# Second attention of a two-block model: seven of eighteen key tiles as float32 products, the other eleven split from PSUM

## Chip, cores and metric

The kernel runs on one NeuronCore of a Trainium2 chip. The metric is the time of one execution on the device, in microseconds (us); for the kernel before it is the median of three runs.

## What is computed

The model has two blocks over 2048 tokens of width 1024, all in float32. Block 1 joins a latent attention and a state space part. Block 2 joins a grouped-query attention with a retention and ends in a mixture of 32 experts. Only the attention of block 2 matters here: 8 query heads of width 64 share 2 key heads, and each query looks at 256 context keys and 2048 token keys, which is 2304 keys or 18 tiles of 128.

```python
def _attend(q, k, v):
    qb = jnp.moveaxis(q.reshape(B, nb, Q_BLOCK, ATTN_KV_HEADS, GQA_GROUP, HEAD_DIM), 1, 0)
    scale = HEAD_DIM ** -0.5
    def one_block(q_blk):
        s = jnp.einsum('bqhgd,bkhd->bhgqk', q_blk, k).astype(jnp.float32) * scale
        p = jax.nn.softmax(s, axis=-1)
        return jnp.einsum('bhgqk,bkhd->bqhgd', p.astype(v.dtype), v)
```

## The kernel before

Stages run one after another: `phase_a`, `phase_qkv`, `phase_attn1` (613 to 1262 us), the state space part's output and `Mix`, `phase_b` (projections of block 2), `phase_attn2` (about 2108 to 3190 us), `phase_out2`, `phase_moe`, `phase_end`.

Most products run in a format called float32r, which keeps the upper bits of a float32 and takes one pass over TensorE. A float32 operand is therefore split in a high part (a cast) and a low part (the operand less its high part, by a subtraction), and a product is put together from the passes that matter. A product of two plain float32 operands is also possible; the profile records it as two MATMUL instructions, each with a weight load of its own.

`Attention2` works through 32 units. A unit is 128 queries of the four heads that share keys, so its moving operands have 512 columns. For each unit:

- `top` finds the maxima of the next unit's scores: 20 products `pa` (16 of 512 columns, 4 of 256, L1161), each reduced by VectorE out of PSUM into `nm` (L1162, two buffers of `pa`). Then a small reduction `mx`, four transposes into a bank of the pool `a2t` and a ScalarE copy make a row of `qm`, which the scores of the next unit need.
- For each of the 18 key tiles, `scores` makes two products into a PSUM tile `ps` (L1182, L1183; two buffers). `exps` takes the exponential on ScalarE from PSUM into an SBUF tile `p` (L1187) and casts it to the high part `ph`, also on ScalarE (L1191). `rest` subtracts to get the low part `pl` (L1199): nine tiles on VectorE, nine on GpSimd. All three operands lie in SBUF.
- The sums over the keys are the softmax's denominators. The string `ACC` says how the high parts enter them. For ten tiles TensorE multiplies `ph` by a column of ones (L1236). For the other eight VectorE adds `ph` to `accD`, seven additions per unit (L1209); `fold` splits the result in `sumh` (ScalarE) and `suml` (VectorE, L319), and two more products with ones bring it in.
- `values` comes five tiles later (`LAG`): `o` += (high and low parts of the values) times `ph` (L1232), and `o1` += (ones, high parts of the values) times `pl` (L1238). Row 0 of `o1` gathers the sum.
- `finish` takes `o` and `o1` out of PSUM (one buffer each, L1247 to L1250), sends the sum through memory to get its reciprocal onto all rows, and multiplies on GpSimd (L1254, L1265).

In the gaps, `Retention.steps` takes one step at the tiles named in `SIDE`, four in a unit. Each step uses a bank of the pool `a2t`, which has two. A chunk's steps include four small VectorE operations with SBUF operands in a row, twice: `rst` at L1049 and `on` at L1076. There are 16 chunks.

PSUM has eight banks, and the stage uses all: `pa` 2, `ps` 2, `o` and `o1`, `a2t` 2. The order of instructions on each engine is made by a planner that follows the order of the code but fills in what it holds to be ready; each engine then works its own queue strictly in order.

Of the kernel before, what the change touches and what calls it, by code (L numbers as in the profile page):

```python
# [10 lines left out]
F = mybir.dt.float32  # L11
R = mybir.dt.float32r
# [3 lines left out]
OP = mybir.AluOpType  # L16
# [17 lines left out]
class K:  # L34
    """What every part of the kernel shares: the core, the arguments, constants, small helpers."""
# [27 lines left out]
    def tr(self, out, x):  # L63
        """out = x transposed, bit for bit."""
        self.nc.tensor.transpose(out, x, self.ident)  # L65

    def rsqrt(self, out, src, n):
        """out = (src / n + eps) ** -0.5 on small tiles."""
        nc = self.nc
        nc.vector.tensor_scalar(out, src, 1.0 / n, EPS, op0=OP.mult, op1=OP.add)  # L70
        w = out.free_size()
        nc.gpsimd.tensor_tensor(out, out, self.mhalf[: out.partition_size(), :w], op=OP.pow)  # L72

    def reduce_angle(self, x, k):
        """x -> x - 2 pi round(x / 2 pi), within [-pi, pi]; k: room of x's shape."""
# [8 lines left out]
    def sin_cos(self, pool, s, c, x, shape):  # L84
        """s, c = sin(x), cos(x); x is spent."""
# [8 lines left out]
    def cmul(self, pool, ore, oim, are, aim, bre, bim, shape, neg_im=False, second=None):  # L94
        """(ore + i oim) = a b, elementwise; with neg_im, oim = -Im(a b)."""
# [16 lines left out]
# Chunks of 16 tokens. Lanes of the tables: (direction, state). A table of powers has 17 entries e:  # L112
# lambda^e forward, lambda^(16 - e) backward.
# [3 lines left out]
def early(k):  # L117
    """What rests on the parameters alone, in small parts."""
# [56 lines left out]
        # Powers 0..16, ascending for both directions: [lanes, e, g].  # L175
# [16 lines left out]
        # Bbar = (lambda_bar - 1) / lambda B  # L192
# [18 lines left out]
        # Tables with e in the direction's order; pw: lambda^s' forward, lambda^(15 - s') backward.  # L211
# [10 lines left out]
        # Bbar with columns (direction, h), zero off its direction.  # L222
# [10 lines left out]
        # The skip weights, on the diagonal of lag 0: rows 32 j + h of a batch of two groups.  # L233
# [72 lines left out]
def mm3(nc, out, lh, ll, rh, rl, start, stop):  # L306
    """out (+)= (lh + ll)^T (rh + rl) in three passes; the product of the low parts is below float32."""
# [5 lines left out]
def split(nc, hi, lo, src, eng=None):  # L313
    """src = hi + lo exactly, each of 12 bits."""
# [13 lines left out]
class Proj:  # L328
    """Rows of a normalized matrix, transposed and split, against weights that stream through."""
# [18 lines left out]
    def half_block(self):  # L348
        """Room of up to two tiles, in that of the last block's low parts."""
# [4 lines left out]
    def add_rows(self, blk, i, x):  # L354
        """Tile i of four of a block: x [128 rows, 1024]."""
# [8 lines left out]
    def weights(self, c0, n, w=None, upto=8):  # L364
        """Columns of the weights, split; w: the rows that are there already."""
# [12 lines left out]
    def rows(self, blk, i, w, n):  # L378
        """PSUM [128 rows of tile i, n]."""
# [6 lines left out]
    def cols(self, blk, w, m):  # L386
        """PSUM [128 columns of weight tile m, 512 rows]."""
# [7 lines left out]
def norm_rows(k, pool, out, x, g, n, b=None):  # L395
    """out = x / rms(x) * g (+ b) over n columns."""
# [73 lines left out]
def rope_tables_1(k):  # L470
    """[c, s, (cos, cos)] and [c, s, (-sin, sin)] of 32 frequencies, to memory. Yields after each small part."""
# [140 lines left out]
class Attention:  # L612
    """For each head and 128 queries: scores with the queries on partitions, their maximum, the
    exponentials, their transposes split in two; for 256 queries the products with the values
    (stationary). The parts of neighbouring tiles of queries alternate as `order` says."""
# [25 lines left out]
    def start(self, n):  # L641
        """The tile n of queries and what it holds."""
# [20 lines left out]
    def M(self, t, j):  # L663
        """The scores times -scale, in place, and the running minimum."""
# [43 lines left out]
    def D(self, t, g, copy=None):  # L708
        """A group that stays whole, for products in float32."""
# [6 lines left out]
    def Y(self, t, g):  # L716
        """Split from the copy: the high part here, the low part on the engine that has time."""
# [6 lines left out]
    def P(self, b):  # L724
        """A share of a block's products with the values."""
# [22 lines left out]
    def X(self, b):  # L748
        """One over the sums, on all partitions."""
# [39 lines left out]
class Attention1(Attention):  # L789
# [4 lines left out]
    def setup(self, ctx):  # L794
        k, nc = self.k, self.nc
        k.at = k.scratch("at", [4, 128, S])            # normalized outputs, features on partitions
# [4 lines left out]
        # The next phase's loads go to the room of the even heads, which is free first.  # L801
# [9 lines left out]
    def load_part(self, h, c):  # L811
        """One of eight parts of a head's keys and values, if it isn't there yet."""
# [78 lines left out]
def decay_tables(k):  # L891
    """Tables of the decays, to memory: the retention's fac, gc, dm and gn. Yields after each small part."""
    nc, a = k.nc, k.a
    k.dec = k.scratch("dec", [128, 9 * HR + 2 * HR + HR * 128])
    with ExitStack() as ctx:
# [4 lines left out]
        # log of the decays: -log(1 + exp(-x)), as min(x, 0) - log(1 + exp(-|x|)).  # L900
# [12 lines left out]
        # Distances on partitions: p + 1, 128 - p, 127 - p, p; and 255 - p, 127 - p, p, 128 + p.  # L913
# [5 lines left out]
        # Factors [128, head, direction]: of the queries; of the keys, with 1/8; of the context's keys.  # L919
# [7 lines left out]
        # Over a chunk, on the state's partitions (direction, dk).  # L927
# [4 lines left out]
        # Decays of the scores [key j, head, query i], with 1/8.  # L932
# [20 lines left out]
class Retention:  # L953
    def constants(self, k, cp):
        """Tables of the decays."""
        self.k = k
        k.rsb = k.scratch("rsb", [NT, 64, 512])        # states of the backward direction before each chunk
        k.ruf = k.scratch("ruf", [NT, 64, 512])        # what each chunk adds to the forward state
# [3 lines left out]
    def spread(self, wk, x, j, name):  # L962
        """[row, head, direction, 64]: x [row, (head, 64)] times factor j."""
# [128 lines left out]
class Attention2:  # L1092
# [92 lines left out]
    def exps(self, u, t):  # L1185
# [4 lines left out]
        if self.HI[t] == "A":  # L1190
            self.nc.scalar.copy(hi, p)  # L1191
# [1287 lines left out]
```

## Time and profile before

| | us |
|---|---|
| median of three runs | 4474.56 |
| lowest and highest of them | 4474.19, 4477.1 |
| span of the profiled execution | 4460.7 |
| median less span | 13.9 |
| TensorE busy over the span | 4063.1 |
| VectorE busy | 3244.0 |
| ScalarE busy | 2301.0 |
| GpSimd busy | 1988.3 |

The page gives busy times of the whole span. The stage of the second attention is about a quarter of it, so the views that count are those of this stretch alone: from the first handing over of a unit's sum (2168.9 us) to the last (3190.6 us) there are 31 units. The profile records the matmuls' ends by a model, so that durations of matmuls that follow each other overlap; the distance between their starts says what one costs.

### The profile page before, as it was taken

To read this page: it belongs to the slowest core of one execution; us is meant where nothing else is said; L and a number is where in the kernel's file an instruction comes from. 1 tells how busy PE (TensorE), PEld (TensorE's weight loads), DVE (VectorE), ACT (ScalarE), POOL (GpSimd) and SP (SyncE) were. 2 spreads that over 40 slices of the span, in tenths; PEclk is the share of its full clock that TensorE was granted. 3 is DMA by queue.
4 is the path that set the end of the run, shared out by engine and by line. 5 is a ranking of instruction groups with operands and counts; after the bars stand their busy time and mean duration, and the time that the engine had idled before them with its cause. 6 is when DMAs were issued, how large, how long until landed. Compare 5 with 4: busy or idle time off the path is not lost. (4 is left out here: it accounts for less than half of the span.)

```text
span 4460.7 us, 60030 instructions
## 1 busy us (share of the span) xinstructions
PE 4063.1 (91%) x19842; PEld 3214.7 (72%) x19842; DVE 3244.0 (73%) x5326; ACT 2301.0 (52%) x4166; POOL 1988.3 (45%) x2239
## 2 busy tenths in 40 slices
PE   7999889999988989999888888989898799999997
PEld 5777768888876878887666666666587677777775
DVE  7563368887625365534999999999765778888886
ACT  3233455555524343322667777777521556666664
POOL 3430078882003422222555555555300566666664
PEclk9999989999998999999999999999999899999998
DMA  5543852331253464334421111110352788888885
GB/s 142 169 146 109 280 192 74 92 112 53 66 160 123 132 206 127 121 103 135 117 71 52 50 45 43 50 41 25 96 172 95 265 279 280 284 280 275 277 282 184
DMA packets 432999, 647.63 MB, mean 145 GB/s; under 512 B 88576, under 2 KB 228096, under 8 KB 432428
## 3 DMA queue, kind: packets, MB, share of 16 engines
q1 hardware_dynamic: 403868, 562.67, 39.9%
q0 software_dynamic: 21840, 66.25, 4.2%
q10 hardware_dynamic: 6976, 14.85, 1.0%
q8 instruction: 157, 2.57, 0.2%
q14 instruction: 158, 1.29, 0.1%
HBM read 496.33 MB, written 156.10 MB: 146 GB/s over the span
## 5 line engine op out<-in xcount | busy, mean ns | idle before, releaser
L1199 POOL TENSOR_TENSOR pl<-p,ph 128x512 fp32r<-128x512 f32 x288 | 416.1, 1450 | 244.8 <-ACT ph L1191 189.4
L2251 DVE TENSOR_TENSOR wlo<-raw,whi 128x1024 fp32r<-128x1024 f32 x256 | 471.6, 1855 | 66.1 <-ACT whi L2248 66.0
L2248 ACT CAST whi<-raw 128x1024 fp32r<-128x1024 f32 x384 | 394.9, 1048 | 130.9 <-DMA raw<-in_moe_w_up 43.9
L1162 DVE TENSOR_REDUCE nm<-pa 128x1 f32<-128x512 f32 (+1 forms) x640 | 390.0, 623 | 19.7 <-PE pa L1161 18.4
L1187 ACT ACTIVATE p<-ps 128x512 f32<-128x512 f32 x576 | 333.2, 599 | 105.6 <-PE ps L1183 87.0
L1161 PE MATMUL pa<-kk,q 128*128 128x512 f32 (+1 forms) x640 | 266.3, 425 | 95.7 <-DVE nm L1162 85.1
L1191 ACT CAST ph<-p 128x512 fp32r<-128x512 f32 x576 | 342.6, 624 | 7.7
L2251 POOL TENSOR_TENSOR wlo<-raw,whi 128x1024 fp32r<-128x1024 f32 x128 | 319.6, 2504 | 53.5 <-ACT whi L2248 47.4
L310 PE MATMUL z<-wh,hlo 128*128 128x512 f32 (+2 forms) x816 | 304.7, 374 | 0.0
L308 PE MATMUL z<-wh,hhi 128*128 128x512 f32 (+2 forms) x768 | 291.4, 381 | 7.5 <-DVE zo L455 2.4
L309 PE MATMUL z<-wl,hhi 128*128 128x512 f32 (+2 forms) x768 | 289.4, 377 | 2.7 <-DVE wl L319 2.7
L72 POOL TENSOR_TENSOR nr<-nr,mhalf 128x1 f32<-128x1 f32 x98 | 61.7, 631 | 499.2 <-DVE nr L70 441.1
L1199 DVE TENSOR_TENSOR pl<-p,ph 128x512 fp32r<-128x512 f32 x288 | 275.4, 956 | 9.8 <-ACT ph L1191 8.3
L1161 PEld LDWEIGHTS pa<-kk,q 128*128 128x128 f32 x640 | 124.0, 195 | 198.4 <-DVE nm L1162 167.0
L1182 PE MATMUL ps<-q,kk 128*128 128x512 f32 x576 | 241.5, 420 | 0.3
L661 PE MATMUL s<-kn,q 128*128 128x512 f32 x768 | 230.0, 407 | 10.0 <-ACT p L674 5.7
L1238 PE MATMUL o<-pl,v 128*128 128x512 f32 x544 | 220.4, 409 | 17.3 <-DVE pl L1199 12.6
L1232 PE MATMUL o<-ph,v 128*128 128x512 f32 x576 | 233.0, 407 | 2.7 <-DVE oc L1249 2.5
L1183 PE MATMUL ps<-qm,kl 65*128 65x512 f32 x576 | 229.0, 407 | 0.2
L1209 DVE TENSOR_TENSOR accD<-accD,ph 128x512 f32<-128x512 f32 x192 | 224.7, 1170 | 0.3
L693 ACT CAST ph<-pt 128x512 fp32r<-128x512 f32 x256 | 142.8, 596 | 151.1 <-PE pt L65 147.8
L697 DVE TENSOR_TENSOR pl<-pt,ph 128x512 fp32r<-128x512 f32 x256 | 167.9, 685 | 67.4 <-ACT ph L693 66.8
(634 smaller groups left out, 11924.5 us busy)
## 6 DMA issues: line engine op xcount, KB each, us to landing
raw<-in_moe_w_gate SPq DMA_DIRECT2D x128, 512.0 KB
raw<-in_moe_w_up SPq DMA_DIRECT2D x128, 512.0 KB
raw<-in_moe_w_down SPq DMA_DIRECT2D x128, 512.0 KB
raw<-in_w_in SPq DMA_DIRECT2D x136, 256.0 KB
w<-in_w_ada SPq DMA_DIRECT2D x96, 256.0 KB
xt<-in_x SPq DMA_DIRECT2D x32, 512.0 KB
xt<-x SPq DMA_DIRECT2D x28, 512.0 KB
rv<-rv SPq DMA_DIRECT2D x34, 256.0 KB
```

The costliest lines, as they stand in the source:

```text
L308: nc.tensor.matmul(out, lh, rh, start=start, stop=False)
L309: nc.tensor.matmul(out, lh, rl, start=False, stop=False)
L310: return nc.tensor.matmul(out, ll, rh, start=False, stop=stop)
L1161: nc.tensor.matmul(pa[:, :c1 - c0], q[:, h], kk[:, c0:c1], start=True, stop=True)
L1162: nc.vector.tensor_reduce(nm[:, h, c:c + 1], pa[:, :c1 - c0], axis=AX.X, op=OP.max)
L1182: nc.tensor.matmul(ps, kk[:, ts], q, start=True, stop=False)
L1187: self.nc.scalar.activation(p, u["s"].pop(t), AF.Exp, scale=self.scale)
L1191: self.nc.scalar.copy(hi, p)
L1199: (nc.vector if self.LO[t] == "D" else nc.gpsimd).tensor_tensor(lo, p, hi.bitcast(F), op=OP.subtract)
L1232: nc.tensor.matmul(u["o"], v[:, t, 64:], hi, start=first, stop=last)
L2248: nc.scalar.copy(hi, raw)
L2251: i = eng.tensor_tensor(lo, raw, hi.bitcast(F), op=OP.subtract)
```

## The change

Seven key tiles, `WHOLE2`, keep their exponentials whole. Their `p` meets the values in one float32 product, with ones and values side by side as the stationary operand (`vw`), so that sum and output come from the same product. There is no cast, no subtraction and no addition for them.

The other eleven, `SPLIT2`, write their exponential back into the PSUM tile it came from. The cast reads PSUM, and the subtraction, now always on VectorE, reads PSUM and the high part. The high parts of these tiles are added up on GpSimd (`acc`, ten additions per unit), and one float32 product with a stationary operand of 128 columns (ones in the first, zeros elsewhere) brings the sum into `o1`. The products with single columns of ones, `accD` and `fold` go.

PSUM is dealt out anew: `ps` has three buffers, `a2t` one. `TOP` moves the three places where two maxima's products fall into one tile. `phase_b` writes the values of the seven tiles whole (64 columns) and those of the others split, into two scratch tensors, which the stage loads with one more transfer per key head.

```diff
+WHOLE2 = (2, 4, 7, 9, 12, 14, 17)
+SPLIT2 = tuple(t for t in range(NT + 2) if t not in WHOLE2)
 class Attention2:
-    TOP = (1, 1, 1, 1, 2, 1, 1, 1, 2, 1, 1, 1, 2, 1, 1, 1, 1, 1)
+    TOP = (1, 1, 1, 2, 1, 1, 2, 1, 2, 1, 1, 1, 1, 1, 1, 1, 1, 1)
-    HI = "AAAAAAAAAAAAAAAAAA"
-    LO = "DPDPDPDPDPDPDPDPDP"
-    ACC = "EDEDEDEDEDEDEDEDEE"      # which one adds up the high parts
-    ROW = "A"
...
-        self.pS = ctx.enter_context(k.pool("a2s", 2, space=PSUM))
+        self.pS = ctx.enter_context(k.pool("a2s", 3, space=PSUM))
-        self.pT = ctx.enter_context(k.pool("a2t", 2, space=PSUM))
+        self.pT = ctx.enter_context(k.pool("a2t", 1, space=PSUM))
-        self.ones = cp.tile([128, 1], R, name="on1")
-        nc.vector.tensor_copy(self.ones, k.ones[:, 0:1])
+        self.one = cp.tile([128, 128], F, name="on1")
+        nc.vector.memset(self.one, 0.0)
+        nc.vector.memset(self.one[:, 0:1], 1.0)
...
-            v = cp.tile([128, self.NK, 192], R, name=f"v{g}")         # ones, high and low parts
+            v = cp.tile([128, len(SPLIT2), 192], R, name=f"v{g}")
+            vw = cp.tile([128, len(WHOLE2), 128], F, name=f"vw{g}")
...
+            nc.sync.dma_start(vw[:, :, 64:], k.v2w[g].rearrange("t p n -> p t n"))
-            nc.gpsimd.tensor_copy(v[:, :, 0:64], k.ones[:, None, 0:64].to_broadcast([128, self.NK, 64]))
+            nc.gpsimd.tensor_copy(v[:, :, 0:64], k.ones[:, None, 0:64].to_broadcast([128, len(SPLIT2), 64]))
+            nc.gpsimd.tensor_copy(vw[:, :, 0:64], k.ones[:, None, 0:64].to_broadcast([128, len(WHOLE2), 64]))
...
     def exps(self, u, t):
-        p = self.wk.tile([128, 512], F, name="p", bufs=5)
-        self.nc.scalar.activation(p, u["s"].pop(t), AF.Exp, scale=self.scale)
+        ps = u["s"].pop(t)
+        if t in WHOLE2:
+            u["p"][t] = p = self.wk.tile([128, 512], F, name="p", bufs=5)
+            self.nc.scalar.activation(p, ps, AF.Exp, scale=self.scale)
+            return
+        self.nc.scalar.activation(ps, ps, AF.Exp, scale=self.scale)
         hi = self.wk.tile([128, 512], R, name="ph", bufs=self.RING)
-        u["p"][t] = [p, hi]
-        if self.HI[t] == "A":
-            self.nc.scalar.copy(hi, p)
+        self.nc.scalar.copy(hi, ps)
+        u["p"][t] = ps, hi
 
     def rest(self, u, t):
...
+        if t in WHOLE2:
+            return
+        ps, hi = u["p"][t]
         lo = self.wk.tile([128, 512], R, name="pl", bufs=self.RING)
-        (nc.vector if self.LO[t] == "D" else nc.gpsimd).tensor_tensor(lo, p, hi.bitcast(F), op=OP.subtract)
+        nc.vector.tensor_tensor(lo, ps, hi.bitcast(F), op=OP.subtract)
         u["p"][t] = hi, lo
...
-                acc = had[0] if had[1] else self.wk.tile([128, 512], F, name="acc" + e, bufs=1)
-                eng.tensor_tensor(acc, had[0], hi.bitcast(F), op=OP.add)
-                u["acc"][e] = acc, True
-            if t == max(self.ACC.rfind(x) for x in "DP"):
-                self.fold(u)
...
+        if t == SPLIT2[0]:
+            u["acc"] = hi.bitcast(F)
+        else:
+            acc = u["acc"] if t > SPLIT2[1] else self.wk.tile([128, 512], F, name="acc")
+            nc.gpsimd.tensor_tensor(acc, u["acc"], hi.bitcast(F), op=OP.add)
+            u["acc"] = acc
 
     def values(self, u, t):
...
-        nc.tensor.matmul(u["o"], v[:, t, 64:], hi, start=first, stop=last)
-        if first:
-            nc.tensor.matmul(u["o1"], v[:, t, 0:128], lo, start=True, stop=False)
-        for x in ([hi] if self.ACC[t] == "E" else []) + (u["sum"] if last and "sum" in u else []):
-            nc.tensor.matmul(u["o1"][0:1], self.ones, x, start=False, stop=False)
-        if not first:
-            nc.tensor.matmul(u["o1"], v[:, t, 0:128], lo, start=False, stop=last)
+        if last:
+            nc.tensor.matmul(u["o1"], self.one, u["acc"], start=False, stop=False)
+        if t in WHOLE2:
+            nc.tensor.matmul(u["o1"], vw[:, WHOLE2.index(t)], p, start=False, stop=last)
+        else:
+            hi, lo = p
+            j = SPLIT2.index(t)
+            nc.tensor.matmul(u["o"], v[:, j, 64:], hi, start=first, stop=t == SPLIT2[-1])
+            nc.tensor.matmul(u["o1"], v[:, j, 0:128], lo, start=first, stop=last)
...
     def do_kv(z, s):
-            vt = wk.tile([128, 2, 2, 64], R, name="vt")
...
+            if kt in WHOLE2:
+                vw = wk.tile([128, 2, 64], F, name="vt")
+                nc.scalar.copy(vw, v)
+                nc.sync.dma_start(k.v2w[:, WHOLE2.index(kt)].rearrange("h p n -> p h n"), vw)
+            else:
+                vt = wk.tile([128, 2, 2, 64], R, name="vt")
+                split(nc, vt[:, :, 0], vt[:, :, 1], v)
```

## Rows read from the trace of the kernel before

**Rows 1.** The page: span, busy time of each engine, VectorE in 40 slices.
```profile
span 4460.7 us, 60030 instructions
...
PE 4063.1 (91%) x19842; PEld 3214.7 (72%) x19842; DVE 3244.0 (73%) x5326; ACT 2301.0 (52%) x4166; POOL 1988.3 (45%) x2239
...
DVE  7563368887625365534999999999765778888886
```
**Rows 2.** One line's instructions: count; ns min/median/max; first and last start.
```profile
L1248 DVE COPY ow<-o x32: 669/672/680, 2168.9 to 3190.6; 1x512 f32<-1x512 f32 x32
```
**Rows 3.** Stretch by engine: us; PE, PEld, DVE, ACT, POOL busy; clock; DMA; GB/s.
```profile
2168.90:3190.60 1021.70, 907.02 (x3985) 631.31 (x3983) 996.08 (x1579) 745.34 (x1388) 570.56 (x398) 0.97 0.18 49
```
**Rows 4.** Groups in that stretch: count | busy us, mean ns | idle before, its releasers.
```profile
L1199 POOL TENSOR_TENSOR pl<-p,ph 128x512 fp32r<-128x512 f32 x278 | 401.5, 1449 | 239.9 <-ACT ph L1191 184.5 <-PE pa L1161 34.8 <-PE o L1238 15.5
L1191 ACT CAST ph<-p 128x512 fp32r<-128x512 f32 x554 | 329.8, 624 | 7.6
L1187 ACT ACTIVATE p<-ps 128x512 f32<-128x512 f32 x554 | 320.7, 599 | 97.7 <-PE ps L1183 80.2 <-POOL pl L1199 8.0 <-PE pa L1161 2.4
...
L1162 DVE TENSOR_REDUCE nm<-pa 128x1 f32<-128x512 f32 x476 | 320.3, 676 | 8.5 <-PE pa L1161 7.8
L1199 DVE TENSOR_TENSOR pl<-p,ph 128x512 fp32r<-128x512 f32 x277 | 263.2, 950 | 9.7 <-ACT ph L1191 8.3
...
L1209 DVE TENSOR_TENSOR accD<-accD,ph 128x512 f32<-128x512 f32 x186 | 218.6, 1175 | 0.3
...
L1076 DVE TENSOR_SCALAR on<-on,mv,r 128x128 f32<-128x128 f32 x64 | 51.2, 850 | 1.6 <-POOL r L72 1.6
...
L1209 DVE TENSOR_TENSOR accD<-ph 128x512 f32<-128x512 f32 x31 | 33.4, 1079 | 0.0
...
L319 DVE TENSOR_TENSOR suml<-accD,sumh 128x512 fp32r<-128x512 f32 x31 | 21.8, 702 | 0.0
```
**Rows 5.** Waits in that stretch: engine, line, waited for: us, times, longest.
```profile
PEld pa L1161 <- DVE nm L1162: 156.8, 196, 4.2
PE pa L1161 <- DVE nm L1162: 82.2, 89, 3.8
```
**Rows 6.** Matmuls in order of time, a run of eleven starts: start us, us.
```profile
2955.14 0.40 PE L1183 MATMUL ps<-qm,kl 65*128 65x512 f32 x1
...
2957.46 0.39 PE L1182 MATMUL ps<-q,kk 128*128 128x512 f32 x1
```
**Rows 7.** Float32 products: timeline of one with 512 columns, of two with 128.
```profile
680.96 1.02 PE L1569 MATMUL pz<-acc,ones 128*1 128x512 f32 x2
...
2913.03 0.39 PE L1060 MATMUL pt<-rv,sm 128*128 128x128 f32 x2
2913.25 0.39 PE L1061 MATMUL pt<-rst,qxt 128*128 128x128 f32 x2
```
**Rows 8.** Instructions of L1569, as in Rows 2.
```profile
L1569 PE MATMUL pz<-acc,ones x32: 590/590/591, 681.0 to 1101.3; 128*1 128x512 f32 x32
```
**Rows 9.** A subtraction from PSUM, in the first attention, as in Rows 2.
```profile
L697 DVE TENSOR_TENSOR pl<-pt,ph x256: 671/683/693, 643.0 to 1259.0; 128x512 fp32r<-128x512 f32 x128
```
**Rows 10.** The first attention's stretch by engine, columns as in Rows 3.
```profile
613.00:1262.00 649.00, 631.69 (x3906) 542.63 (x3907) 508.79 (x1103) 347.13 (x864) 376.01 (x920) 0.98 0.28 83
```
**Rows 11.** A burst on VectorE and TensorE after it, in order of time.
```profile
2927.71 4.14 DVE L1076 TENSOR_SCALAR on<-on,mv,r 128x128 f32<-128x128 f32 x4
...
2932.24 0.51 PE L1161 MATMUL pa<-kk,q 128*128 128x512 f32 x1 [2.61 <-DVE nm L1162]
...
2933.73 0.63 PE L1182 MATMUL ps<-q,kk 128*128 128x512 f32 x1
2934.16 0.63 PE L1183 MATMUL ps<-qm,kl 65*128 65x512 f32 x1
```
**Rows 12.** TensorE at the border of two units, in order of time.
```profile
2940.18 0.40 PE L1236 MATMUL o<-ph,on 128*1 128x512 f32 x1
2940.67 0.60 PE L65 MATMUL pt<-ident,mx 128*1 128x128 f32 x4
```

More of the change, by code (lines that the diff above doesn't have):

```diff
@@ L1169, in top @@
             self.k.tr(pt[0:1, h], mx[:, h:h + 1])
-        if self.ROW == "D":
-            nc.vector.tensor_scalar(qm[64:65], pt[0:1], -1.0, None, op0=OP.mult)
-        else:
-            nc.scalar.mul(qm[64:65], pt[0:1], -1.0)
+        nc.scalar.mul(qm[64:65], pt[0:1], -1.0)
         yield
@@ L1185, in exps @@
     def exps(self, u, t):
-        p = self.wk.tile([128, 512], F, name="p", bufs=5)
-        self.nc.scalar.activation(p, u["s"].pop(t), AF.Exp, scale=self.scale)
+        ps = u["s"].pop(t)
[4 more added lines that the diff above has]
+        self.nc.scalar.activation(ps, ps, AF.Exp, scale=self.scale)
         hi = self.wk.tile([128, 512], R, name="ph", bufs=self.RING)
-        u["p"][t] = [p, hi]
-        if self.HI[t] == "A":
-            self.nc.scalar.copy(hi, p)
+        self.nc.scalar.copy(hi, ps)
+        u["p"][t] = ps, hi
     def rest(self, u, t):
         nc = self.nc
-        p, hi = u["p"][t]
-        if self.HI[t] == "D":
-            nc.vector.tensor_copy(hi, p)
+        if t in WHOLE2:
+            return
+        ps, hi = u["p"][t]
         lo = self.wk.tile([128, 512], R, name="pl", bufs=self.RING)
-        (nc.vector if self.LO[t] == "D" else nc.gpsimd).tensor_tensor(lo, p, hi.bitcast(F), op=OP.subtract)
+        nc.vector.tensor_tensor(lo, ps, hi.bitcast(F), op=OP.subtract)
         u["p"][t] = hi, lo
-        e = self.ACC[t]
-        if e in "DP":
-            eng = nc.vector if e == "D" else nc.gpsimd
-            had = u["acc"].get(e)
-            if had is None:
-                u["acc"][e] = hi.bitcast(F), False
-            else:
-                acc = had[0] if had[1] else self.wk.tile([128, 512], F, name="acc" + e, bufs=1)
-                eng.tensor_tensor(acc, had[0], hi.bitcast(F), op=OP.add)
-                u["acc"][e] = acc, True
-            if t == max(self.ACC.rfind(x) for x in "DP"):
-                self.fold(u)
-    def fold(self, u):
-        nc = self.nc
-        accs = [x[0] for x in u["acc"].values()]
-        for x in accs[1:]:
-            nc.vector.tensor_tensor(accs[0], accs[0], x, op=OP.add)
-        u["sum"] = [self.wk.tile([128, 512], R, name="sum" + n, bufs=1) for n in "hl"]
-        split(nc, *u["sum"], accs[0])
+        if t == SPLIT2[0]:
[4 more added lines that the diff above has]
+            u["acc"] = acc
     def values(self, u, t):
@@ L1229, in values @@
             u["o1"] = self.pO.tile([128, 512], F, name="o1")
-        v = self.kv[u["n"] % 2][2]
-        hi, lo = u["p"].pop(t)
-        nc.tensor.matmul(u["o"], v[:, t, 64:], hi, start=first, stop=last)
-        if first:
-            nc.tensor.matmul(u["o1"], v[:, t, 0:128], lo, start=True, stop=False)
-        for x in ([hi] if self.ACC[t] == "E" else []) + (u["sum"] if last and "sum" in u else []):
-            nc.tensor.matmul(u["o1"][0:1], self.ones, x, start=False, stop=False)
-        if not first:
-            nc.tensor.matmul(u["o1"], v[:, t, 0:128], lo, start=False, stop=last)
+        v, vw = self.kv[u["n"] % 2][2:]
+        p = u["p"].pop(t)
+        if last:
[7 more added lines that the diff above has]
+            nc.tensor.matmul(u["o1"], v[:, j, 0:128], lo, start=first, stop=last)
     def finish(self, u):
@@ L1278, in run @@
                 if t == 0:
-                    us[n] = dict(n=n, p={}, s={}, acc={})
+                    us[n] = dict(n=n, p={}, s={})
                     for _ in ahead:
@@ L1634, in phase_b @@
     k.k2 = k.scratch("k2", [2, 2, 128, NK * 128])
-    k.v2 = k.scratch("v2", [2, NK, 128, 128])
+    k.v2 = k.scratch("v2", [2, len(SPLIT2), 128, 128])
+    k.v2w = k.scratch("v2w", [2, len(WHOLE2), 128, 64])
     k.rq = k.scratch("rq", [NT, 128, 256])
@@ L1715, in do_kv @@
             kt = (s + 2) % (NT + 2)
-            vt = wk.tile([128, 2, 2, 64], R, name="vt")
             v = z[:, 128:256].rearrange("p (n c) -> p n c", c=64)
-            split(nc, vt[:, :, 0], vt[:, :, 1], v)
-            nc.sync.dma_start(k.v2[:, kt].rearrange("h p n -> p h n"), vt.bitcast(F).rearrange("p h a n -> p h (a n)"))
+            if kt in WHOLE2:
[5 more added lines that the diff above has]
+                split(nc, vt[:, :, 0], vt[:, :, 1], v)
+                nc.sync.dma_start(k.v2[:, SPLIT2.index(kt)].rearrange("h p n -> p h n"),
+                                  vt.bitcast(F).rearrange("p h a n -> p h (a n)"))
             def late():
```

2 lines of the change are left out of this document (1 added, 1 removed).

## The prediction

> **What bounds the kernel now.** Read the page first: over the whole span TensorE looks busiest and VectorE comes second, but the slices of VectorE show one place where it is full, slices 20 to 28 of 40 [rows 1]. That is the second attention, so everything is worked out from that stretch. Its beat is read from one instruction that comes once per unit: 31 intervals in 1021.7 us [rows 2], 32.96 us per unit. In the view by engine VectorE is busy 996.08 us of it, 97.5%, or 32.1 us per unit; TensorE 88.8%, ScalarE 73%, GpSimd 56% [rows 3]. The waits say the same from the other side: TensorE's loads wait 156.8 us and its matmuls 82.2 us for `nm`, the reduction by which VectorE frees a `pa` buffer [rows 5], while VectorE's largest group waits 8.5 us [rows 4]. So VectorE sets the beat, TensorE waits for it, and the other two have room.
>
> TensorE's 88.8% must not be taken for its load. Eleven matmuls start within 2.32 us [rows 6], 0.232 us apart, though each is drawn 0.39 to 0.40 us long. By starts a unit costs, before: 100 matmuls of 512 columns (36 scores, 16 maxima, 36 values, 12 sums), 23.2 us; 4 of 256 columns at half, 0.46; and 3985 / 31 = 128.5 records less these 104 leave 24.5 short ones (retention, transposes) at 0.11 us (two records in 0.22 us [rows 7]), 2.7. Sum 26.4 us, 80% of the beat. The Trainium skill, "Perfetto Trace Analysis", section "Identifying the Most-Contended Engine", says that matmul busy time is not a good measure of how close TensorE is to its limit. The trace agrees: 0.40 us drawn, 0.232 us apart.
>
> **The change, part by part, per unit.**
>
> *VectorE.* Removed: 277 subtractions (263.2 us), 186 + 31 additions (218.6 and 33.4), 31 of `suml` (21.8) [rows 4], 537.0 us / 31 = 17.3 us. Added: 11 subtractions that read PSUM. The trace before has that form in the first attention, 683 ns with a maximum of 693 [rows 9], while GpSimd was busy 376 of 649 us there [rows 10]; the present ones, with both operands in SBUF, take 950 [rows 4]. I take 683, since the operands are the same as there: 7.5 us; upper end 10.5. Net -9.8 us, less about 0.5 because neighbours overlap by some 0.08 us and there are six fewer: VectorE falls from 32.1 to 22.8 us (up to 25.8). The Trainium skill, "SBUF — State Buffer", section "Who interferes with whom", says that a VectorE instruction with two SBUF inputs contends with a GpSimd one that reads SBUF, and one with at most one SBUF input doesn't. The 950 against 683 ns agree; by that rule the lower price holds, without it the upper one.
>
> *TensorE.* Removed: 14 matmuls on the values and 12 on the sums, 26 x 0.232 = 6.0 us. Added: 7 + 1 float32 products of 512 columns. One such product is two records; together they are drawn 1.02 us [rows 7] and each 0.590 [rows 8], so the second starts 0.43 after the first and a product takes 0.86 us. That row has a stationary operand of one column; the 128-column ones run at 0.11 us per 128 columns and record [rows 7], which is 0.88 us for 512, so wider weights don't show. 8 x 0.86 = 6.9 us. TensorE: 26.4 - 6.0 + 6.9 = 27.3 us. This is a step the wrong way, and TensorE becomes the fullest engine.
>
> *ScalarE.* 24.0 us before (745.34 / 31). Away: seven casts at 624 ns and `sumh`, 5.0 us. Eleven exponentials now write PSUM, which no row shows on this engine. The nearest are 599 ns from PSUM to SBUF and 624 from SBUF to SBUF [rows 4]; I take 0.60 and bound it by 0.55 and 0.75, so -0.6 to +1.7 us. ScalarE ends near 19 us, at most 21, with 6 us to spare: nothing on the path.
>
> *GpSimd.* 570.56 / 31 = 18.4 us before. Away 9 subtractions at 1.45 us, 13.0; added 10 additions with the same operands, 14.5 at that price and less if VectorE's two-input work no longer blocks them. About 19 to 20 us, covered by TensorE's 27. The additions form a chain, but the product that needs `acc` comes five tiles after the last high part, about 8 us, and three additions in a row are 4.4. If GpSimd fell behind by more, TensorE would wait at that one product.
>
> *Longer hold of the scores.* A `ps` tile of the eleven is now free only after the cast and the subtraction, and TensorE's next scores are queued behind that, with the values and maxima after them. Shortest hold: two matmuls 0.46, some 0.16 for the end of the last (0.39 drawn less 0.232), 0.60, 0.62, 0.68: 2.5 us. Three buffers at 1.7 us per tile allow about 5. The cover is 2.5 us of waiting in queues; a burst on VectorE can use it up.
>
> *The rest.* One bank of `a2t` instead of two: retention's steps lie two tiles or more apart (over 3 us), and ScalarE or VectorE empty a bank in about that, so 0 to 0.5 us. `TOP` keeps its sum of 21. `phase_b` loses 7 small subtractions, each below the 683 ns of a fourfold width, so 0 to 5 us in all if they were on the path; I take 0, since the same tiles keep their split of the keys and their rotation on VectorE. The loads go through SP's queue at the start of the stage, one transfer more per key head with fewer bytes; the tiles they bring are needed two tiles later than the first. I take 0, with a microsecond or two on either side.
>
> **What is late next.** TensorE needs 27.3 us, so losses that were free under VectorE now count:
> - Bursts on VectorE. Four small operations `on` took 4.14 us in a row; TensorE ran out of buffers and idled 2.61 us, and afterwards its matmuls started 0.43 us apart, the lower clock level, where 0.232 is the upper one [rows 11]; some nine such matmuls lose another 1.9 us. On average a burst is 51.2 / 16 = 3.2 us [rows 4]. With 1.5 us of cover that is 1.7 us idle and half the time the clock, 2.6 us for each of 16 bursts: 1.3 per unit.
> - The border of units, where maxima, transposes and a ScalarE copy follow each other: 0.49 us between starts, 0.26 of them idle [rows 12], and about as much again after the copy. In a stage without slack I take 0.7.
> - The single buffers of `o` and `o1`, between last use and copies: 0.5. Other: 0.5.
> Sum 3.0, so the beat is 30.3 us. As a check on the losses, the first attention, whose TensorE is drawn busy 97.3% of its stretch [rows 10], keeps no more than 3% open, which would put the beat near 28.1; that stage has no such bursts. The gain is (32.96 - 30.3) x 32 = 85 us. From the profiled execution's 4460.7 us that is 4375.7; the median lies 13.9 us above that execution, so 4390.
>
> **The rivals.**
> 1. *TensorE runs nearly without gaps* (beat 28.5). For: VectorE keeps 4 us free, the planner fills borders with retention. Against: the bursts stay. Gain 143 us: 4332.
> 2. *Bursts cost fully*: 4.5 us for each of 16 (2.25 per unit), 1.4 at the border, 0.5 and 0.8 elsewhere: beat 32.2. For: the longer hold of `ps` ties TensorE to VectorE more tightly than before. Gain 24 us: 4450.
> 3. *TensorE is already full.* If the drawn 88.8% were real load, 29.3 us, the change would add 0.9 and the losses 3.0: beat 33.2, no change, 4474 to 4482. Against: the starts 0.232 us apart. This is the reading which the rule on matmul busy time warns of.
> 4. *The hold of the scores decides, and the kernel is slower.* With a hold of H for split tiles and 2.5 us for whole ones, three buffers give a beat of (11 H + 17.5) / 3. It equals today's 32.96 at H = 7.4 us, that is with 4.9 us of queueing per split tile, every time. At 8.0 it is 35.2, and 32 x 2.2 = 70 us more: 4545. For: cast and subtraction wait in two strict queues, and the subtraction stands behind the next tile's reduction. Against: ScalarE and VectorE each keep over a fifth of the beat free.
> That the change doesn't do what it says would need float32 products at twice their price, which the rows of two widths exclude.
>
> **How the numbers follow.** Chances: forecast (beat 29.4 to 31.4) 0.50; rival 1 0.16; rival 2 0.19; rival 3 0.06; rival 4 0.09. The range takes in the forecast and rivals 1 and 2, and leaves out 3 and 4: 4330 to 4455. A measurement of this kernel can tell a change of about 0.2%, 9 us, from none. Faster by more: 0.85; within: 0.06; slower: 0.09.
>
> **What would show it.** In the stretch from the first `ow` to the last: 31 intervals of 30.3 us; VectorE busy near 75% and no longer first; the subtraction at 683 ns with a narrow spread; the two records of a float32 product 0.43 us apart; TensorE's waits for `nm` down, those for `pl` (freeing `ps`) new but below a microsecond per unit. Wrong would be: VectorE still above 95%; or `scores` waiting longest, for `pl`, which is rival 4; or exponentials into PSUM well above 0.75 us.

## The result, and the profile after

| | before | after | forecast |
|---|---|---|---|
| median, us (four runs each, on one chip) | 4475.83 | 4366.4 | 4390 (4330 to 4455) |
| lowest and highest, us | 4474.19, 4482.13 | 4362.52, 4376.58 | |
| ratio, 95% interval | | 0.9754 (0.9739 to 0.9769) | |
| beat of the stage, us per unit | 32.96 | 29.63 | 30.3 |
| VectorE busy, us per unit | 32.1 | 23.3 | 22.8 |
| ScalarE busy, us per unit | 24.0 | 19.6 | 19 |
| GpSimd busy, us per unit | 18.4 | 17.2 | 19 to 20 |

The change makes the kernel 2.5% faster, by 109 us; the forecast said 85. First the page of the changed kernel: span, busy time of each engine and VectorE in 40 slices, as in [rows 1].

```profile
span 4374.8 us, 58926 instructions
...
PE 4053.6 (93%) x19522; PEld 3214.0 (73%) x19522; DVE 2960.5 (68%) x5128; ACT 2160.2 (49%) x3910; POOL 1953.6 (45%) x2273
...
DVE  7664258887644447544588788778565888888886
```

The row of nines is gone: in the second attention VectorE stands at 7 and 8. The instruction that comes once per unit, beside [rows 2] (count; ns minimum, median, maximum; first and last start):

```profile
L1243 DVE COPY ow<-o x32: 669/678/679, 2181.2 to 3099.6; 1x512 f32<-1x512 f32 x32
```

And the stretch between its first and last start, beside [rows 3] (us; busy time of TensorE, its weight loads, VectorE, ScalarE, GpSimd; granted clock; DMA; GB/s):

```profile
2181.20:3099.60 918.40, 876.67 (x3678) 615.34 (x3677) 722.89 (x1392) 606.50 (x1140) 533.23 (x428) 0.98 0.20 54
```

31 intervals in 918.4 us are 29.63 us, 3.33 less than before; times 32 that is 107 us of the 109. Taken from the start of `phase_b`'s last product to the last `ow`, the stage went from 1082.9 to 973.1 us, 109.8 less. (The two profiled spans differ by only 85.9. In every run that lists both, the time is 1.8 us above the span; so the profiled execution of before, at 4460.7, ran some 12 us under its kernel's median, and that of after, 4376.58, 10 us over its own. After is already 19 us later at the first store of `x1`, in code that the change leaves alone.)

The groups of that stretch that answer to [rows 4]: count | busy us, mean ns | idle before, and its releasers.

```profile
L1212 POOL TENSOR_TENSOR acc<-acc,ph 128x512 f32<-128x512 f32 x278 | 355.9, 1280 | 187.0 <-ACT ph L1196 182.5
...
L1205 DVE TENSOR_TENSOR pl<-ps,ph 128x512 fp32r<-128x512 f32 x339 | 229.9, 683 | 39.2 <-ACT ph L1196 36.1
...
L1076 DVE TENSOR_SCALAR on<-on,mv,r 128x128 f32<-128x128 f32 x64 | 35.2, 611 | 7.4 <-POOL r L72 7.4
```

The subtraction out of PSUM costs 683 ns, the price of [rows 9] to the nanosecond, where the one out of SBUF cost 950. The third line was not in the forecast: the small operations `on`, whose code is the same, fell from 850 to 611 ns. The waits of that stretch (engine, line, waited for: us, times, longest), beside [rows 5]:

```profile
PEld pa L1167 <- DVE nm L1168: 48.8, 94, 4.0
...
PE pa L1167 <- DVE nm L1168: 21.0, 8, 3.2
...
PEld ps L1185 <- DVE pl L1205: 12.3, 37, 0.8
```

TensorE waited 239.0 us for `nm` and now waits 69.8; the new wait, that of the scores for `pl`, is 12.3 us in the whole stage. The operations that [rows 4 and 8] priced only from afar, over the stage:

```profile
L1228 PE MATMUL o<-p,vw x448: 590/592/595, 2154.9 to 3098.9; 128*128 128x512 f32 x150
...
L1194 ACT ACTIVATE ps<-ps x352: 573/582/609, 2145.7 to 3094.0; 128x512 f32<-128x512 f32 x176
...
L1192 ACT ACTIVATE p<-ps x224: 590/602/649, 2147.7 to 3095.1; 128x512 f32<-128x512 f32 x112
```

A float32 record takes as long with 128 columns of weights (592 ns) as with one [rows 8]. The exponential into PSUM is 20 ns shorter than into SBUF, inside the bounds.

### The profile page after: what moved, and what is told of

Read it like the earlier page. It is cut to its first block, busy times and chain, and to the rows that moved or that the text cites. A ratio compares the mean times of both kernels' runs of the same rounds, so it can differ in the third digit from the quotient of the medians.

```text
span 4374.8 us, 58926 instructions
## 1 busy us (share of the span) xinstructions
PE 4053.6 (93%) x19522; PEld 3214.0 (73%) x19522; DVE 2960.5 (68%) x5128; ACT 2160.2 (49%) x3910; POOL 1953.6 (45%) x2273
## 5 line engine op out<-in xcount | busy, mean ns | idle before, releaser
L1212 POOL TENSOR_TENSOR acc<-acc,ph 128x512 f32<-128x512 f32 x288 | 368.7, 1280 | 192.3 <-ACT ph L1196 187.6
L1167 PE MATMUL pa<-kk,q 128*128 128x512 f32 (+1 forms) x640 | 307.4, 489 | 31.4 <-DVE nm L1168 23.3
L1194 ACT ACTIVATE ps<-ps 128x512 f32<-128x512 f32 x352 | 204.5, 586 | 182.1 <-PE ps L1186 149.7
L1205 DVE TENSOR_TENSOR pl<-ps,ph 128x512 fp32r<-128x512 f32 x352 | 238.7, 683 | 43.2 <-ACT ph L1196 40.0
L1185 PE MATMUL ps<-q,kk 128*128 128x512 f32 x576 | 251.2, 437 | 0.3
L1228 PE MATMUL o<-p,vw 128*128 128x512 f32 x448 | 228.9, 592 | 0.0
L739 PE MATMUL o<-ph,v 128*128 128x256 f32 x1024 | 215.8, 292 | 0.2 <-ACT ph L693 0.2
L1196 ACT CAST ph<-ps 128x512 fp32r<-128x512 f32 x352 | 202.7, 588 | 17.3 <-ACT ps L1194 0.4
L661 PEld LDWEIGHTS s<-kn,q 128*128 128x128 f32 x768 | 141.8, 192 | 54.1 <-ACT p L674 6.3
```

What stands on the lines that cost most here:

```text
L661: self.nc.tensor.matmul(sp[:, c - c0:e - c0], l, r, start=n == 0, stop=n == len(ops) - 1)
L1167: nc.tensor.matmul(pa[:, :c1 - c0], q[:, h], kk[:, c0:c1], start=True, stop=True)
L1185: nc.tensor.matmul(ps, kk[:, ts], q, start=True, stop=False)
L1205: nc.vector.tensor_tensor(lo, ps, hi.bitcast(F), op=OP.subtract)
L1212: nc.gpsimd.tensor_tensor(acc, u["acc"], hi.bitcast(F), op=OP.add)
```

## Experiments

The theory: VectorE set the beat; relieved, it leaves TensorE's load by starts (27.2 us) plus losses in which TensorE waits for bursts elsewhere. Against it stand rival 3 (TensorE was already full) and rival 4 (the hold of the scores decides). Each edit is to the kernel after, except the first. "Load" is TensorE's, by starts. The expectations number the runs in their own way: their e3 is experiment 3 here, e4 is 6, e6 is the five tiles of 7, e9 is 8 and e10 the first half of 9.

**1. VectorE relieved alone.** In the kernel before, all sums go to products with ones; VectorE loses its seven additions and `suml`, TensorE gains six products.

```diff
-    ACC = "EDEDEDEDEDEDEDEDEE"
+    ACC = "EEEEEEEEEEEEEEEEEE"
```

> The kernel before with one edit: all 18 high parts meet the column of ones on TensorE, so VectorE's seven additions, its subtraction for the sum and ScalarE's cast go; nothing else of the change. My theory (VectorE set the beat of 32.96 us, TensorE's real load was 26.4): VectorE loses 273.8 us / 31 = 8.8 us a unit, TensorE gains 8 products less 2, 6 x 0.232 = 1.4, load 27.8, with 2.4 us of losses a beat of 30.2 and a time near 4387. Rival 3 (TensorE was already full at its drawn 88.8%): the beat grows by 1.4 to 34.4 and the time to 4521.

Measured: 4392.33 us, ratio 0.9808 (0.9792 to 0.9825), beat 30.35.

```profile
2182.60:3123.60 941.00, 895.55 (x4171) 643.57 (x4169) 740.73 (x1330) 750.60 (x1355) 535.18 (x397) 1.00 0.20 53
```

TensorE got more products and the beat fell by 2.6 us, so TensorE was not full and rival 3 falls. VectorE is down to 740.73 / 31 = 23.9 us. One string brings some 85 of the 109 us, without any float32 product or exponential in PSUM.

**2. The hold of the scores.** `ps` back to two buffers, `a2t` to two.

```diff
-        self.pS = ctx.enter_context(k.pool("a2s", 3, space=PSUM))
+        self.pS = ctx.enter_context(k.pool("a2s", 2, space=PSUM))
-        self.pT = ctx.enter_context(k.pool("a2t", 1, space=PSUM))
+        self.pT = ctx.enter_context(k.pool("a2t", 2, space=PSUM))
```

> The changed kernel with two score buffers and two banks for retention, as before the change. If the hold of the scores decides (rival 4), the beat is inverse to the number of buffers: 29.63 x 3 / 2 = 44 us, time near 4830. If it doesn't, a hold of about 3.5 us for split and 2.0 for whole tiles asks for (11 x 3.5 + 7 x 2.0) / 2 = 26 us, less than TensorE needs; beat 29.6 to 30.6, time 4366 to 4400.

Measured: 4385.18 us (one time), beat 30.17. Its waits from 2180 to 3060 us:

```profile
PEld ps L1185 <- ACT p L1192: 60.9, 164, 0.8
...
PEld ps L1185 <- DVE pl L1205: 28.7, 74, 1.6
```

The scores now do wait, but 1.6 us at most. With two buffers the prediction's formula reads (11 H + 17.5) / 2 = 30.17, so H is at most 3.9 us, far from the 7.4 of rival 4, which falls. Going back costs 0.5 us of the beat, in one run: what the third score buffer gives, less what the second bank of `a2t` would.

**3. The subtraction out of SBUF.** The same split tiles, but the exponential goes to SBUF, and cast and subtraction read it there.

```diff
-        self.nc.scalar.activation(ps, ps, AF.Exp, scale=self.scale)
+        p = self.wk.tile([128, 512], F, name="p", bufs=7)
+        self.nc.scalar.activation(p, ps, AF.Exp, scale=self.scale)
...
-        self.nc.scalar.copy(hi, ps)
-        u["p"][t] = ps, hi
+        self.nc.scalar.copy(hi, p)
+        u["p"][t] = p, hi
```

> The changed kernel with the exponentials of the eleven split tiles in SBUF again: cast and subtraction read SBUF, on the same engines. My theory (two SBUF inputs contend with GpSimd): the subtraction goes from 683 to 850-950 ns, GpSimd's additions from 1281 to 1350-1450, VectorE from 23.3 to about 26 us a unit, still below TensorE, so the beat moves by 0 to +0.7 us (4366 to 4390). Rival (the longer hold in PSUM costs more than the contention saves): the beat falls by 0.3 to 1 us (4335 to 4357).

Measured: 4468.41 us (one time), beat 32.53: nearly the kernel before, 102 us above after. This is the widest miss of the study. The stretch by engine:

```profile
2180.20:3188.60 1008.40, 904.39 (x3678) 617.88 (x3676) 864.83 (x1392) 616.83 (x1140) 602.78 (x428) 0.97 0.18 49
```

The subtraction's durations (minimum, median, maximum):

```profile
L1206 DVE TENSOR_TENSOR pl<-p,ph x352: 654/714/5295, 2149.8 to 3183.6; 128x512 fp32r<-128x512 f32 x176
```

Its group (busy us, mean ns):

```profile
L1206 DVE TENSOR_TENSOR pl<-p,ph 128x512 fp32r<-128x512 f32 x339 | 387.5, 1150 | 19.7 <-ACT ph L1197 18.0
```

And the waits:

```profile
PEld pa L1167 <- DVE nm L1168: 153.1, 175, 5.2
...
PE pa L1167 <- DVE nm L1168: 81.9, 84, 4.4
```

VectorE is busy 864.83 / 31 = 27.9 us of 32.53, so it is not full, and yet TensorE waits 235 us for it. The median of the subtraction is 714 ns, the mean 1150, the longest 5295. That one in the order of time, with the GpSimd instructions around it and TensorE's next start (start us, us):

```profile
2899.57 5.29 DVE L1206 TENSOR_TENSOR pl<-p,ph 128x512 fp32r<-128x512 f32 x1
...
2899.54 1.30 POOL L1261 TENSOR_TENSOR oc<-oc,rb 64x512 f32<-64x512 f32 x1
2900.79 1.29 POOL L1213 TENSOR_TENSOR acc<-acc,ph 128x512 f32<-128x512 f32 x1
2902.03 1.06 POOL L966 TENSOR_TENSOR qx<-rq,decays 128x512 f32<-128x512 f32 x1
2903.03 2.95 POOL L1213 TENSOR_TENSOR acc<-acc,ph 128x512 f32<-128x512 f32 x2
...
2905.51 0.39 PE L1167 MATMUL pa<-kk,q 128*128 128x256 f32 x1 [3.01 <-DVE nm L1168]
```

The subtraction begins 0.03 us after GpSimd's `oc` and ends at 2904.86 us, only after that, an addition, `qx` and a further addition, the first of the two in the last GpSimd line. The reductions behind it on VectorE are late, and TensorE idles 3.01 us. So what two SBUF operands cost is not a somewhat longer instruction each time: half stay under 0.72 us, while 149 of the 352 took over 1 us, 27 over 2 and 8 over 3, and these hold up the engine.

**4. The same without GpSimd's additions.** As in 3, and the sums of the eleven tiles go to products with a column of ones.

```diff
-            nc.gpsimd.tensor_tensor(acc, u["acc"], hi.bitcast(F), op=OP.add)
...
-            nc.tensor.matmul(u["o1"], self.one, u["acc"], start=False, stop=False)
...
+            nc.tensor.matmul(u["o1"][0:1], self.ones, hi, start=False, stop=False)
```

> The kernel of e3 (cast and subtraction from SBUF) without GpSimd's additions: the eleven high parts meet a column of ones on TensorE instead, 11 x 0.232 - 0.86 = 1.7 us more of its load, 28.9 us a unit. If GpSimd's additions are what slowed e3's subtractions (1139 ns on average, up to 5.3 us), they take 683 ns again, TensorE's waits for the maxima fall, and the beat falls from 32.5 to about 31.3 in spite of the load, time near 4425. If the way over SBUF is slow by itself, the subtractions stay above 900 ns and the beat rises to about 34, time near 4515.

Measured: 4373.26 us (one time), beat 29.71. The stretch by engine:

```profile
2169.90:3091.00 921.10, 911.19 (x3956) 626.67 (x3954) 699.90 (x1392) 632.60 (x1140) 153.27 (x120) 1.00 0.20 54
```

Two of its groups:

```profile
L1205 DVE TENSOR_TENSOR pl<-p,ph 128x512 fp32r<-128x512 f32 x339 | 246.8, 732 | 26.3 <-ACT ph L1196 24.9
...
L1076 DVE TENSOR_SCALAR on<-on,mv,r 128x128 f32<-128x128 f32 x64 | 17.9, 343 | 11.2 <-POOL r L72 11.2
```

With GpSimd nearly empty the same subtraction out of SBUF takes 732 ns on average instead of 1150, and `on` takes 343 ns instead of 594. TensorE's load rose by 1.7 us to 28.9 and the beat still fell by 2.8 against experiment 3, leaving 0.8 us of losses. So the way over SBUF is not slow by itself, and the loss of 3 goes with VectorE and GpSimd meeting. Both expectations, of 3 and of 4, were too small for the same reason: they count the longer instruction and not what waits behind it.

**5. The additions on VectorE.** All of `acc` moves from GpSimd.

```diff
-            nc.gpsimd.tensor_tensor(acc, u["acc"], hi.bitcast(F), op=OP.add)
+            nc.vector.tensor_tensor(acc, u["acc"], hi.bitcast(F), op=OP.add)
```

> The changed kernel with the ten additions of high parts on VectorE in place of GpSimd. My theory (the room on VectorE is what the change gains): VectorE's load goes from 23.3 by 10 x 0.60 to 0.68 to about 29.5 to 30 us a unit, as GpSimd is then nearly idle and the additions are not held up; with losses a beat of 31 to 32, time 4410 to 4445. Rival (the sums' place doesn't matter while TensorE sets the beat): 29.6, time 4358 to 4374.

Measured: 4434.07 us (one time), beat 31.77, VectorE 867.20 / 31 = 28.0 us. The time is as expected: the place of the additions is worth 2.1 us per unit, again with VectorE short of full. How the loss comes about is another matter. Some waits of TensorE, and the additions themselves:

```profile
PEld ps L1185 <- ACT p L1192: 57.2, 149, 1.2
PE pa L1167 <- DMA q<-q: 39.6, 26, 3.4
...
PEld pa L1167 <- DMA q<-q: 20.1, 11, 3.1
PEld pa L1167 <- DVE nm L1168: 19.1, 67, 0.9
...
L1212 DVE TENSOR_TENSOR acc<-acc,ph 128x512 f32<-128x512 f32 x279 | 203.5, 729 | 0.0
```

TensorE's loads wait less for `nm` than in after (19.1 us instead of 48.8), and more for the exponentials and for the next unit's queries (59.7 us instead of 21.0). The expectation named no such wait, and no run separates these.

**6. The bursts.** The four `on` of a chunk move to ScalarE, with one small VectorE operation for the bias.

```diff
+            nb = wk.tile([128, HR], F, name="nb")
+            nc.vector.scalar_tensor_tensor(nb, mv[:, :, 0], -1.0, r4, op0=OP.mult, op1=OP.mult)
...
-                nc.vector.tensor_scalar(on[:, h], on[:, h], mv[:, h, 0:1], r4[:, h:h + 1], op0=OP.subtract, op1=OP.mult)
+                nc.scalar.activation(on[:, h], on[:, h], AF.Identity, scale=r4[:, h:h + 1], bias=nb[:, h:h + 1])
```

> The changed kernel with retention's four normalizations per chunk moved from VectorE to ScalarE (a small product for the bias stays on VectorE), so that the bursts leave VectorE. My theory (bursts stall TensorE, 2 us or more for each of 16): beat from 29.63 to about 29.0, time 4340 to 4352. Rival (the bursts are covered by the buffers): within 8 us of 4366, as ScalarE gains 1.8 us a chunk and has room.

Measured: 4344.07 us, ratio 0.9698 (0.9677 to 0.9718), beat 28.92, as expected. The waits for `nm`, 69.8 us in after:

```profile
PEld pa L1169 <- DVE nm L1170: 37.2, 98, 1.9
...
PE pa L1169 <- DVE nm L1170: 7.6, 9, 1.0
```

The longest of them went from 4.0 to 1.9 us. So the bursts cost after 0.7 us per unit, 22 us in all. What such a burst is can be seen in after at 2408 us, beside [rows 11]; the first line is another chunk's, with GpSimd idle:

```profile
2357.94 1.12 DVE L1076 TENSOR_SCALAR on<-on,mv,r 128x128 f32<-128x128 f32 x4 [0.46 <-POOL r L72]
...
2408.04 4.25 DVE L1076 TENSOR_SCALAR on<-on,mv,r 128x128 f32<-128x128 f32 x4 [0.21 <-POOL r L72]
...
2407.97 1.29 POOL L1212 TENSOR_TENSOR acc<-acc,ph 128x512 f32<-128x512 f32 x1
2409.22 1.26 POOL L1260 TENSOR_TENSOR oc<-oc,rb 64x512 f32<-64x512 f32 x1
2410.44 1.25 POOL L1212 TENSOR_TENSOR acc<-acc,ph 128x512 f32<-128x512 f32 x1
...
2412.95 0.79 PE L1167 MATMUL pa<-kk,q 128*128 128x512 f32 x1 [3.00 <-DVE nm L1168]
2413.54 0.63 PE L1185 MATMUL ps<-q,kk 128*128 128x512 f32 x1
2413.96 0.63 PE L1186 MATMUL ps<-qm,kl 65*128 65x512 f32 x1
```

The same four operations take 1.12 us or, through three GpSimd instructions in a row, 4.25. TensorE idles 3.00 us, and its next matmuls start 0.42 us apart, the lower clock level (granted clock 0.50 from 2412.9 to 2416 us).

**7. How many tiles stay whole.** Nine, then five. A whole tile costs TensorE 0.86 us instead of 0.46, and spares VectorE, ScalarE and GpSimd an operation each.

```diff
-WHOLE2 = (2, 4, 7, 9, 12, 14, 17)
+WHOLE2 = (2, 4, 6, 8, 10, 12, 14, 16, 17)
```

> The changed kernel with nine whole tiles (2, 4, 6, 8, 10, 12, 14, 16, 17) and nine split ones. TensorE's load grows by 2 x (0.86 - 0.464) = 0.8 us a unit, VectorE's falls by 2 x 0.6 = 1.2. My theory (TensorE's load plus about 2.4 us of losses is the beat): 29.63 + 0.8 = 30.4, time near 4391. Rival (what VectorE, ScalarE and the hold of the scores leave open is the beat): it falls by 0.3 to 0.6 us, time near 4350.

```diff
-WHOLE2 = (2, 4, 7, 9, 12, 14, 17)
+WHOLE2 = (2, 5, 9, 13, 17)
```

> The changed kernel with five whole tiles (2, 5, 9, 13, 17) and thirteen split ones. TensorE's load falls by 0.8 us a unit to 26.4, VectorE's grows by 1.2 to 24.5, GpSimd's by 2.6 to 19.8. My theory (TensorE's load plus constant losses): beat 28.8, time near 4341. Rival (fuller VectorE and ScalarE give the gain back as losses): beat 29.6 or above, time 4366 or above.

| whole tiles | load | beat | losses | GpSimd | ratio, 95% interval |
|---|---|---|---|---|---|
| 9 | 28.0 | 29.53 | 1.5 | 14.7 | 0.9746 (0.9724 to 0.9768) |
| 7 (after) | 27.2 | 29.63 | 2.4 | 17.2 | 0.9754 (0.9739 to 0.9769) |
| 5 | 26.4 | 30.37 | 4.0 | 19.8 | 0.9814 (0.9791 to 0.9836) |

My theory missed both times, and with five the rival's outcome came: I had taken the losses as constant, and they rise as GpSimd fills (and with it VectorE and ScalarE). Nine and seven can't be told apart; five is slower although TensorE has least to do. In the groups of five, `on` is back at 867 ns:

```profile
L1076 DVE TENSOR_SCALAR on<-on,mv,r 128x128 f32<-128x128 f32 x64 | 51.6, 867 | 5.4 <-POOL r L72 5.4
```

And in its waits one has grown, that for the queries of the next unit, 57.5 us in all (21.0 in after):

```profile
PEld pa L1167 <- DMA q<-q: 32.5, 21, 5.4
...
PE pa L1167 <- DMA q<-q: 25.0, 16, 5.1
```

**8. Five whole tiles, `on` on ScalarE.** Experiments 6 and 7 together.

> The kernel of e4 (normalizations on ScalarE) with five whole tiles, as in e6. In e6 TensorE's load fell by 0.8 us a unit but the beat rose from 29.63 to 30.37, and the normalizations on VectorE took 867 ns instead of 611. Theory A (e6 lost because VectorE's instructions with SBUF operands were held up by GpSimd's longer runs of additions): without them the smaller load pays, beat 28.92 - 0.8 = 28.1 to 28.5, time 4318 to 4332. Theory B (a fuller VectorE and ScalarE stall TensorE, whatever the reason): the beat rises as it did from the changed kernel to e6, to about 29.6, time near 4367.

Measured: 4352.93 us, ratio 0.9732 (0.9709 to 0.9755), beat 29.18, between the two theories. The bursts are gone and the wait for the queries stays. On SP's queue, which issues their loads, a store of a finished unit stands until GpSimd's `oc`, 135.4 us in all where experiment 6 has 105.6. TensorE's waits, and that of SP's queue:

```profile
PEld pa L1169 <- DMA q<-q: 32.1, 20, 5.5
...
PE pa L1169 <- DMA q<-q: 23.2, 13, 5.2
...
SPq L1264 <- POOL oc L1262: 135.4, 31, 6.7
```

**9. The queries two units ahead.** `q` and `qm` get three buffers and are loaded a unit earlier; first with seven whole tiles and `on` on ScalarE, then with five.

```diff
-        q = self.qp.tile([128, 4, 128], R, name="q")
+        q = self.qp.tile([128, 4, 128], R, name="q", bufs=3)
...
-        qm = self.qp.tile([65, 4, 128], R, name="qm")
+        qm = self.qp.tile([65, 4, 128], R, name="qm", bufs=3)
...
-                        self.q[n + 1] = self.load_q(n + 1)
+                        if n == 0:
+                            self.q[1] = self.load_q(1)
...
+                    if n + 2 < N:
+                        self.q[n + 2] = self.load_q(n + 2)
```

> The kernel of e4 with the queries loaded two units ahead, in three buffers. TensorE's waits for the queries' transfers (11.2 us and more in the stage) go. If they are losses of their own, the beat falls from 28.92 by 0.3 to 0.6, time 4325 to 4335; if another wait at the border of units is late right behind them, the time stays within 5 us of 4344.

> The kernel of e9 (five whole tiles, normalizations on ScalarE) with the queries loaded two units ahead as in e10. In e9 TensorE waited 55 us in the stage for the queries' transfers, which stand on SP's queue behind a store that waits for GpSimd, and GpSimd is fuller with thirteen split tiles. If that queue gave back what the smaller TensorE load should have brought, the beat falls from 29.18 to 27.7-28.5, below e4 and e10, time 4308 to 4332. If a fuller VectorE and ScalarE stall TensorE anyway, other waits grow in its place and the beat stays at 28.7 or above, time 4340 or above.

With seven: 4348.51 us, ratio 0.9718 (0.9697 to 0.9739), beat 28.70; the time is the second outcome expected, not to be told from experiment 6, though the beat fell by 0.2. With five: 4327.99 us, ratio 0.9658 (0.9636 to 0.9681), beat 27.98, as expected.

```profile
2194.70:3062.00 867.30, 843.35 (x3678) 606.66 (x3677) 726.55 (x1406) 666.39 (x1266) 614.35 (x491) 1.00 0.21 57
```

GpSimd is as full as in experiment 8 (19.8 us per unit), TensorE no longer waits for the queries, and 25 us are gone. So their lateness cost that time. That they stood on SP behind what waits for GpSimd fits the 135.4 us of experiment 8, but the edit also gives them a third buffer, and no run separates the two. This version beats both kernels, by 148 us and 38.

Early loading has a price that the beat doesn't show. In both runs TensorE idles 9.8 us between `phase_b`'s last product and the next product of the stage, for a reason that the profile doesn't name. That next product, first with seven whole tiles, then with five:

```profile
2123.51 0.77 PE L1169 MATMUL pa<-kk,q 128*128 128x512 f32 x1 [9.84 <-issue]
...
2135.22 0.77 PE L1169 MATMUL pa<-kk,q 128*128 128x512 f32 x1 [9.81 <-issue]
```

In experiments 6 and 8 TensorE goes on without such a gap. From `phase_b`'s last product to the first `ow` they take 55.9 and 55.4 us, these two 69.0 and 69.7. With seven that eats the 0.2 us per unit; with five the beat gains 37 us and the kernel 25.

## Why the prediction was right

**VectorE as the bound: shown.** Experiment 1 relieves it alone and the beat follows, with TensorE doing more. Part of its 32.1 us was blocked time, though: the addition that took 1175 ns there [rows 4] takes 729 in experiment 5, where GpSimd is nearly idle. What [rows 3 and 5] said was right, and so was the choice to price TensorE by starts: drawn busy 876.67 us, 95.5% of the stretch, it would seem as good as full after, yet with experiment 9 the same stretch is 51 us shorter, 867.3 us.

**The loads.** VectorE 23.3 us (forecast 22.8), ScalarE 19.6 (19), TensorE 27.2 by the same starts (27.3; the distance inside a float32 product is 0.43 us, as forecast). GpSimd was put too high, 17.2 instead of 19 to 20: the ten additions were priced at 1.45 us and took 1.28. It lay off the path.

**The term that was mis-sized: the losses**, 29.63 - 27.2 = 2.4 us instead of 3.0. The bursts were put at 1.3 us per unit; experiment 6 takes them out and the beat falls by 0.7. They had been sized from the kernel before, where `on` took 850 ns; in after it takes 611, a burst 35.2 / 16 = 2.2 us instead of 3.2. With 2.2 the prediction's own working gives 0.7 us idle and half of 1.9, 1.65 for each of 16, or 0.85 per unit. A part that the change does not touch had become cheaper. That accounts for 0.6 us per unit, 19 of the 24 us between forecast and result. What is left, 2.4 - 0.7 = 1.7 us, equals what the prediction gave to the border, the single buffers and the rest together. None of them was measured by itself, and experiment 4, with GpSimd nearly empty, leaves 0.8 us of losses in all, so that this fits may be luck. Why `on` became cheaper is open. With GpSimd nearly empty it is cheap (343 ns in experiment 4), but otherwise it does not follow how busy GpSimd is: experiment 1 keeps the old subtractions on GpSimd and has 596 ns, experiment 3 has 594 with 19.4 us of GpSimd per unit, and five whole tiles have 867 with 19.8. The prediction's check on the losses (3% open in the first attention, so a beat near 28.1) read drawn busy time as load, against which it warns itself: after is drawn busy 95.5%, 4.5% open, and by starts 8% of its beat are losses.

**The upper end for the subtraction was far too low.** The prediction bounded what is lost if the PSUM operand brought no relief by 10.5 instead of 7.5 us of VectorE's load, all of it hidden under TensorE. Experiment 3 measures 2.9 us of the beat, 102 us of the kernel, at 12.5 us of subtractions and a VectorE load of 27.9. The step that failed is pricing contention by the mean of an instruction: the mean is made of ordinary ones and of some that block the engine for up to 5.29 us, of which the two buffers of `pa` and other work covered 2.3 in the case shown, and 1.3 of the 4.25 in experiment 6. The forecast was not hurt, since the lower price held. The Trainium skill, "SBUF — State Buffer", section "Who interferes with whom", has the rule on two SBUF inputs and says that the order of issue decides who blocks. The trace agrees with both (683 against 1150 ns; GpSimd 0.03 us ahead in the case shown), but the block lasted over four GpSimd instructions, where that section speaks of the length of one. The same section of the Trainium skill frees a VectorE instruction with at most one SBUF input only outside the 2-port performance modes, a condition that the prediction left out; `on`, with one full-sized operand in SBUF, is hit here too (1.12 against 4.25 us), and no row shows in which mode it ran.

**The rivals.** 1 (28.5 us) asks for less than 1.3 us of losses, and 2.4 were left; it is about what experiments 6 and 9 reach. 2 took the bursts as dearer where they became cheaper. 3 and 4 fell by experiments 1 and 2.

**What stays open.** Experiment 9 still loses 1.6 us per unit on 26.4 of load, and 9.8 us once at the start. That experiment 3's blocking explains all of its 102 us is read from its waits and from experiment 4, which also moves work to TensorE; no run took the collisions away and nothing else.

## What to carry to other kernels

A burst sized from the old trace is an estimate with a wide range: its cost can shrink (3.2 to 2.2 us here) or grow back (five whole tiles) in code that nobody touched. Where VectorE and GpSimd both read SBUF, ask for the longest instruction and what waits behind it, not for the mean: the gain of moving an operand to PSUM was 102 us where the busy time said it would be hidden. And once TensorE is the bound, count its load and its losses apart: taking work off it made the kernel slower (five whole tiles) until the bursts and the late queries were gone.

## What the runs showed of the hardware

- A VectorE subtraction with two SBUF operands took 5.29 us instead of 0.68 while GpSimd ran four instructions back to back.
- An operation with one full-sized operand in SBUF is hit as well: four `on` took 4.25 us beside three GpSimd instructions and 1.12 without, and one of 128 x 4 elements (L70 of after) averaged 1185 ns where it averaged 154 in the stage before. GpSimd was busy in both; at 2355.77 us it took 1.04 us beside an addition that GpSimd had begun 0.27 us earlier. Its group in after:

```profile
L70 DVE TENSOR_SCALAR r<-mv 128x4 f32<-128x4 f32 x16 | 19.0, 1185 | 0.0
```

- The operations that read PSUM stayed narrow beside the same GpSimd work: 660 to 694 ns.

```profile
L1205 DVE TENSOR_TENSOR pl<-ps,ph x352: 660/681/694, 2150.9 to 3095.3; 128x512 fp32r<-128x512 f32 x176
```
